# Hybrid attention layer on one core: one list of epilogue steps, two vector operations exchanged between engines, earlier weight requests

## The chip, the core and the metric

The kernel runs on one core of a Trainium2 chip. The metric is the device time of one execution in microseconds (us); lower is better. Five queues work side by side: TensorE (PE: matmuls and transposes), VectorE (DVE), ScalarE (ACT), GpSimd (POOL) and SyncE (SP), which here only requests DMA transfers. Each takes its instructions in a fixed order, and an instruction that waits holds up all that stand behind it in its queue.

## The reference, cut to what matters

```python
hdn = rmsnorm(x, norm_gain)                       # x: 2048 tokens x 1024
q_a, k_a, v_a, g_a, q_b, k_b, v_b, g_b = split(hdn @ w_in)
q, k = rope(rmsnorm(q, gain)), rope(rmsnorm(k, gain))      # both mixers, per head
o_a = banded_attention(q_a, k_a, v_a, 127, sinks) * silu(g_a)      # 8 heads, 2 kv heads
o_b = dilated_attention(q_b, k_b, v_b) * silu(g_b)  # 3 patterns, merged by their denominators
out = x + concat(o_a, o_b) @ w_out
```

## The kernel before, in words

The projections run in eight stages (`STAGES`): B0 to B3 (two heads of the dilated mixer each), A0 and A1 (four heads of the window mixer each), O0 and O1 (half the output columns each). A stage goes over the 2048 tokens in four blocks `sb`, a block in two halves of 256 tokens, a half in two tiles `tt` of 128. Every product is made of three matmuls, since weights and activations are split into a high and a low part. `proj` makes q, k and v of a tile in one PSUM tile `pj` (two buffers), then the gates of the half.

After each q/k/v tile, `norm_rope` squares and reduces on ACT and DVE (`un`, L413), multiplies by the cosine and sine tables on DVE out of PSUM (L420 and L422 for B, L427 and L429 for A), adds the two products on POOL (L431, the rotary sum) and, as the last reader of `pj`, writes the low part of V on DVE (L311). After both tiles of a half, `norm_factors` makes the norm factors `fac` on POOL (L437, L182). `norm_split` multiplies the rotated q and k by `fac` on DVE (L447), rounds them on ACT (L456, L457) and subtracts on POOL (L458, L459), which gives `hl`. The transposes of `hl` come in the next half.

The attention work is cut into units of three or four steps (`scores`, `transposes`, `pv`, `after`). `advance` calls the next step, and the loop at the end spreads these calls over the matmuls of the projections by the cost noted with each step. The softmax denominators go to DRAM (`rD`, `rA`) and come back broadcast over the partitions (`Rb`, one buffer); POOL multiplies the attention outputs `osum` with them: `final` for the window mixer (L686, L688), `first`, `second` and `third` for the dilated one (L899, L904, L905, L906). These late pieces stand in the list `late` with a count of `tick` calls, each entry counting by itself.

`w_tiles` loads a stage's weights through three staging buffers (`stg`): `main(c)` and `gate(c)` request a block (L118, L131) and split it on ACT and DVE (L101 and L102, L104 and L105). They are called from the matmul loops of the last half of the stage before.

The order of the program is not the order of the queues. The launch builds the program with

```python
with tile.TileContext(nc, schedule_with_timeline_sim=True) as tc:
```

so that, when it is built, the instructions of each queue are put in order along a simulated timeline; the place in the program then decides between instructions that could both go.

Of the kernel before, what the change touches and what calls it, by code (L numbers as in the profile page):

```python
# [9 lines left out]
F32 = mybir.dt.float32  # L10
# [8 lines left out]
KC = DM // 128  # L19
# [4 lines left out]
SB = 3  # L24
BIG = 1e30
STAGES = [("B", 0), ("B", 1), ("B", 2), ("B", 3), ("A", 0), ("A", 1), ("O", 0), ("O", 1)]

# [6 lines left out]
def hybrid_layer(ctx, tc, xT, xn, x, wB, wA, wO, ng, gains, sinks, rot, masks, ident, out):  # L34
# [72 lines left out]
    def w_tiles(si):  # L107
        kind, idx = STAGES[si]
        src = {"B": wB, "A": wA, "O": wO}[kind][idx]
        nm = 256 if kind == "O" else 384  # L110
        q, g = [], []

        def main(c, then=None):
            if si == 0:
                f = wk.tile([128, nm], F32, name=("cq", "ck", "cv")[c % 3])
            else:
                f = xp.tile([128, nm], F32, name="stg", bufs=SB)
            nc.sync.dma_start(f, src[:, c, :nm])  # L118
            h = wp.tile([128, nm], F32R, name="wh", bufs=WB)
            l = wp.tile([128, nm], F32R, name="wl", bufs=WB)  # L120
            if then:
                then()
            split_w(kind, c, f, h, l)
            q.append((h, l))

        def gate(c):
            k = 2 if kind == "B" else 1
            if c % k:
                return
            f = xp.tile([128, k, 256 // k], F32, name="stg", bufs=SB)  # L130
            nc.sync.dma_start(f, src[:, c:c + k, nm:])  # L131
# [5 lines left out]
        return q, g, main, gate  # L137


# [106 lines left out]
    def proj(si, sb):  # L246
# [22 lines left out]
        for half in range(2):  # L269
# [8 lines left out]
            for tt in range(2):  # L278
# [98 lines left out]
    deferred = []  # L377
    late = []

    tabs = {}  # L380
# [25 lines left out]
    def norm_rope(kind, nq, nk, T, tt, pj, TC, TS, u, vt):  # L406
# [16 lines left out]
        for qk, m in enumerate((nq, nk) if kind == "A" else ()):  # L423
# [17 lines left out]
    def norm_split(kind, nq, nk, t1s, fac):  # L441
# [74 lines left out]
    def proj_out(si, sb, wq, wg, last):  # L516
# [4 lines left out]
        for half in range(2):  # L521
# [6 lines left out]
            for tt in range(2):  # L528
# [6 lines left out]
                for n in range(2 * KC):  # L535
# [5 lines left out]
                    if o == 0:  # L541
                        continue
                    if last and half == 1 and tt == 1:
                        W[si + 1][2](c)
                        W[si + 1][3](c)
# [110 lines left out]
    def units_A(si, sb):  # L656
# [21 lines left out]
        def final(p):  # L678
            d = osum["d", p]
            rb = wk.tile([128, 512], F32, name="Rb", bufs=1)  # L680
            for a in range(2):
                nc.sync.dma_start(rb[64 * a:64 * a + 64, :],
                                  bass.AP(tensor=d.tensor, offset=d.offset + a * 512, ap=[[0, 64], [1, 512]]))
            t = osum[p]
            g = G[si, sb][p].rearrange("p r i u -> p (r i u)")
            nc.gpsimd.tensor_tensor(t, t, g, op=OP.mult)  # L686
            mix = wk.tile([128, 512], F32, name="o1c", bufs=1)
            nc.gpsimd.tensor_tensor(cm_view(mix), cm_view(t), to_cm(rb), op=OP.mult)  # L688
            for a in range(2):
                nc.sync.dma_start(mx[2 * sb + a][:, 2 * idx + p, :], mix[:, 256 * a:256 * a + 256])  # L690

# [7 lines left out]
    def pair_units(si, sb, p, sc, osum, rows, final):  # L699
# [7 lines left out]
        def scores(h):  # L707
            if h % 2 == 0:
                osum[p] = wk.tile([128, 512], F32, name="osum", bufs=3)
            s[h] = window_scores(si, sb, h, [sc[:, 0, h, i:i + 1] for i in range(4)], [sc[:, 1, h, i:i + 1] for i in range(4)])  # L710
# [31 lines left out]
        def after():  # L742
            rows(p)
            late.append([5, lambda: final(p)])

# [4 lines left out]
    def units_B(si, sb):  # L750
        sc = wk.tile([128, 4, 2, 2], F32, name="scB")
        osum = wk.tile([128, 512], F32, name="osum", bufs=3)
        d = spill_tiles(si)
        units = []
        for h in range(2):
            def after(h=h):
                if h == 1:
# [4 lines left out]
                    cs = slice(sb * 128, sb * 128 + 128)  # L762
                    nc.sync.dma_start(d["o"][:, :, cs].rearrange("r p c -> p r c"), osum.rearrange("p (r c) -> p r c", r=4))
            stats = ([sc[:, i, 0, h:h + 1] for i in range(4)], [sc[:, i, 1, h:h + 1] for i in range(4)])
            units.append(window_unit(si, sb, h, stats, cm_view(osum[64 * h:64 * h + 64, :]), after))
# [5 lines left out]
    def units_D(si, r):  # L771
# [4 lines left out]
        def dil(h):  # L776
# [61 lines left out]
            def pv():  # L838
# [11 lines left out]
                if h == 0:  # L850
                    c["o2"] = wk.tile([128, 512], F32, name="osum", bufs=3)
                evac_o(po, c["o2"][hp:hp + 64, :])

            def after():
# [26 lines left out]
                nc.sync.dma_start(dd, rr)  # L881
                o1 = wk.tile([128, 512], F32, name="o1c", bufs=1)
                nc.sync.dma_start(o1, d["o"][r])
                gc = wk.tile([128, 512], F32, name="gc", bufs=1)
                nc.sync.dma_start(gc, d["g"][r])
                o2 = c["o2"]
                def bcast(k):
# [4 lines left out]
                    return rb  # L892

                def first():
                    rb = bcast(0)
                    late.append([3, lambda: second(rb)])

                def second(rb):
                    nc.gpsimd.tensor_tensor(o1, o1, rb, op=OP.mult)  # L899
                    rb = bcast(1)  # L900
                    late.append([3, lambda: third(rb)])

                def third(rb):
                    nc.gpsimd.tensor_tensor(o2, o2, rb, op=OP.mult)  # L904
                    nc.gpsimd.tensor_tensor(o2, o2, o1, op=OP.add)  # L905
                    nc.gpsimd.tensor_tensor(o2, o2, gc, op=OP.mult)  # L906
# [133 lines left out]
```

## Time and profile before

| | |
|---|---|
| median of 3 runs | 1259.9 us (1255.32 to 1261.03) |
| the profiled execution: its time | 1261.51 us |
| the profiled execution: its span | 1259.4 us |
| mean granted clock of TensorE | 0.969 of full speed |
| TensorE busy | 1174.8 us, 8328 matmuls |
| VectorE, ScalarE, GpSimd busy | 850.7, 834.7, 680.4 us |

All durations below are from the profiled execution; the span is 2.1 us shorter than its time. Matmuls overlap, so a busy TensorE is not one at its peak: the count of matmuls in a stretch says more than the busy share. The clock is given as a share of the full 2.4 GHz; a mean between 0.5 and 1 over a stretch means that part of it was granted at 1.2 GHz.

### The profile page before, as it was taken

The page shows a single profiled execution, that of the slowest core. Times are in us where ns is not written, and L with a number is a line of the kernel's source. Part 1 is how long each engine was busy: PE and PEld are TensorE (multiplying, and loading weights), DVE is VectorE, ACT ScalarE, POOL GpSimd, SP SyncE. Part 2 cuts the span into 40 slices and gives each one's busy share as a digit, 9 for nine tenths or more (in the row PEclk, how much of TensorE's full clock was granted, in tenths as well). Part 3 has the DMA queues.
Part 4 walks back from the last instruction along what each step waited for, and adds up shares of the span by engine and source line. Part 5 has one row for each costly group of instructions (what it writes and reads, how often), then busy time and mean ns, then how long its engine had stood idle before and what let it go on. Part 6 is the DMA issues. An engine that isn't in the chain of part 4 may idle for free.

```text
span 1259.4 us, 25438 instructions
## 1 busy us (share of the span) xinstructions
PE 1174.8 (93%) x8328; PEld 1141.3 (91%) x8328; DVE 850.7 (68%) x2288; ACT 834.7 (66%) x2418; POOL 680.4 (54%) x788
## 2 busy tenths in 40 slices
PE   6898979899899798899998999999999999999899
PEld 5898979899799798888997999898899998999898
DVE  5676768678677678776777788789868877522221
ACT  6477868678677687676777677677776776522221
POOL 4886734566645574536576567565655554333122
PEclk9899989999899899899998999999999999999999
DMA  7454677877687667687775764545333225566561
GB/s 215 120 166 127 193 226 212 229 200 212 182 250 207 210 190 201 189 244 204 199 210 172 228 203 143 150 137 167 114 97 94 80 89 165 163 192 211 166 191 69
DMA packets 196883, 220.98 MB, mean 175 GB/s; under 512 B 34312, under 2 KB 143632, under 8 KB 196752
## 3 DMA queue, kind: packets, MB, share of 16 engines
q1 hardware_dynamic: 196752, 219.37, 59.3%
q8 instruction: 66, 1.08, 0.4%
q14 instruction: 65, 0.53, 0.1%
HBM read 164.44 MB, written 54.86 MB: 174 GB/s over the span
## 4 chain that ended last, share of the span: by engine, by line
PE 55%; DMA 16%; DVE 10%; ACT 8%; POOL 6%; issue 3%; SPq 2%; POOLq 0%; ACTq 0%; DVEq 0%
PE pj L244 39%; DMA xs<-in_xT 3%; DMA Rb<-rD 2%; DMA stg<-in_wB 2%; PE po L849 2%; DMA stg<-in_wO 2%; DMA stg<-in_wA 2%; PE sc L590 1%; PE sc L591 1%; PE po L645 1%; PE pt L828 1%; PE po L735 1%; PE pt L719 1%; ACT P L599 1%; DVE ptl L574 1%
## 5 line engine op out<-in xcount | busy, mean ns | idle before, releaser
L244 PE MATMUL pj<-wh,xh 128*128 128x384 f32 (+1 forms) x1008 | 332.8, 332 | 12.2 <-ACT wh L104 5.5
L244 PE MATMUL pj<-wl,xh 128*128 128x384 f32 (+1 forms) x1008 | 334.4, 332 | 0.8 <-DVE wl L102 0.7
L244 PE MATMUL pj<-wh,xl 128*128 128x384 f32 (+1 forms) x1008 | 333.4, 331 | 1.3 <-DVE xl L157 1.3
L157 POOL TENSOR_TENSOR xl<-xs,xh 128x512 fp32r<-128x512 f32 x158 | 210.3, 1341 | 146.3 <-ACT xh L155 136.6
L155 ACT ACTIVATE xh<-xs 128x512 fp32r<-128x512 f32 x252 | 154.5, 629 | 123.6 <-PE pj L244 100.6
L244 PEld LDWEIGHTS pj<-wh,xh 128*128 128x128 f32 x1008 | 194.0, 193 | 15.7 <-ACT wh L104 5.8
L244 PEld LDWEIGHTS pj<-wl,xh 128*128 128x128 f32 x1008 | 194.8, 193 | 3.2 <-DVE wl L102 1.1
L244 PEld LDWEIGHTS pj<-wh,xl 128*128 128x128 f32 x1008 | 194.4, 193 | 3.0 <-DVE xl L157 1.6
L574 DVE TENSOR_TENSOR ptl<-pt,pth 128x512 fp32r<-128x512 f32 (+3 forms) x232 | 142.0, 619 | 35.5 <-ACT pth L573 31.8
L244 PE MATMUL pj<-xh,wgh 128*128 128x256 f32 x496 | 147.7, 298 | 17.9 <-DVE V L311 12.0
L244 PE MATMUL pj<-xh,wgl 128*128 128x256 f32 x496 | 145.8, 294 | 0.0
L244 PE MATMUL pj<-xl,wgh 128*128 128x256 f32 x496 | 145.4, 293 | 0.0
L573 ACT ACTIVATE pth<-pt 128x512 fp32r<-128x512 f32 (+3 forms) x232 | 123.1, 543 | 23.1 <-PE pt L719 8.1
L431 POOL TENSOR_TENSOR t<-t,t 128x256 f32<-128x256 f32 (+1 forms) x96 | 78.1, 814 | 77.9 <-DVE t L422 57.2
L244 PEld LDWEIGHTS pj<-xh,wgh 128*128 128x128 f32 x496 | 97.8, 197 | 19.7 <-ACT klz L502 5.9
L244 PEld LDWEIGHTS pj<-xl,wgh 128*128 128x128 f32 x496 | 97.8, 197 | 0.6
L244 PEld LDWEIGHTS pj<-xh,wgl 128*128 128x128 f32 x496 | 97.4, 196 | 0.9 <-DVE wgl L105 0.2
L814 ACT ACTIVATE P<-P,scD 128x256 f32<-128x256 f32 (+3 forms) x128 | 71.6, 560 | 33.6 <-DVE scD L813 32.9
L157 DVE TENSOR_TENSOR xl<-xs,xh 128x512 fp32r<-128x512 f32 x94 | 76.9, 823 | 21.1 <-ACT xh L155 20.5
L447 DVE TENSOR_TENSOR t<-t,fac 128x256 f32<-128x256 f32 (+1 forms) x96 | 67.4, 710 | 30.8 <-POOL fac L182 23.7
L182 POOL TENSOR_TENSOR fac<-un,mhalf 128x8 f32<-128x8 f32 (+1 forms) x48 | 85.4, 1779 | 2.5
L813 DVE CUSTOM_DVE_ANT_0 P<-sc,mk 128x256 f32<-128x256 f32 (+3 forms) x128 | 61.1, 484 | 32.2 <-PE sc L809 31.5
(188 smaller groups left out, 3082.8 us busy)
## 6 DMA issues: line engine op xcount, KB each, us to landing
xs<-in_xT SPq DMA_DIRECT2D x94, 512.0 KB
xs<-mx SPq DMA_DIRECT2D x32, 512.0 KB
vd<-V SPq DMA_DIRECT2D x64, 128.0 KB
qd<-qc SPq DMA_DIRECT2D x32, 256.0 KB
TT<-tab SPq DMA_DIRECT2D x32, 256.0 KB
cv<-vd SPq DMA_DIRECT2D x32, 256.0 KB
cq<-qd SPq DMA_DIRECT2D x32, 256.0 KB
ck<-kd SPq DMA_DIRECT2D x64, 128.0 KB
```

The source lines that it names most:

```text
L155: nc.scalar.activation(h, f, AF.Copy)
L157: eng.tensor_tensor(l, f, f32(h), op=OP.subtract)
L182: nc.gpsimd.tensor_tensor(y, u, mhalf.to_broadcast([128, n]), op=OP.pow)
L244: nc.tensor.matmul(o, a, b, start=first and n == 0, stop=last and n == 2, skip_group_check=True)
L431: nc.gpsimd.tensor_tensor(t1[:, :n], t1[:, :n], t2[:, :n], op=OP.add)
L447: nc.vector.tensor_tensor(t1v, t1v, fac[:, tt, :, None].to_broadcast([128, nh, 64]), op=OP.mult)
L573: nc.scalar.activation(hi, pt, AF.Copy)
L574: nc.vector.tensor_tensor(lo, pt, f32(hi), op=OP.subtract)
L590: nc.tensor.matmul(sc[:, j, :], q[h // 2][:, h % 2, i, :], kw, start=True, stop=False)
L813: nc.vector.tensor_tensor_reduce(pd, o[:, :m], m2[:, 512 - m:], -0.125, BIG, OP.add, OP.min, nb)
L814: nc.scalar.activation(pd, pd, AF.Exp, bias=nb, scale=-1.0, accum_out=l)
L849: nc.tensor.matmul(po[:, o:o + w], a, b, start=n_ == 0, stop=n_ == len(seq) - 1, skip_group_check=True)
```

## The change

Three edits. (1) The rotary sum L431 goes from POOL to DVE, and the multiplication by `fac` L447 from DVE to POOL. (2) Every attention epilogue becomes an entry of short steps in one list; only the head of the list counts down, one step at a time; the loads of `o1` and `gc` move from `after` into the first step, the stores to `mx` into a last step of their own, two ticks after the last multiplication. `osum_tile` runs steps of the list at once when three `osum` tiles are in use. (3) The request of a weight block is taken out of `main` and `gate`: `prime` requests the first three blocks in the tile before, and each split is followed by the request of the block three further on; the order of the blocks and the three buffers stay.

```diff
+        def load(n):
+            if n >= len(order) or order[n] in staged:
+                return
+            part, c = order[n]
...
+                f = xp.tile(shape, F32, name="stg", bufs=SB)
+            nc.sync.dma_start(f, src[:, c, :nm] if part == "m" else src[:, c:c + k, nm:])
+            staged[order[n]] = f
+        def prime():
+            for n in range(SB):
+                load(n)
         def main(c, then=None):
-            nc.sync.dma_start(f, src[:, c, :nm])
+            f, n = take("m", c)
             h = wp.tile([128, nm], F32R, name="wh", bufs=WB)
...
             split_w(kind, c, f, h, l)
             q.append((h, l))
+            if si:
+                load(n + SB)
...
+                    if last and half == 1 and tt == 0 and c == 3:
+                        W[si + 1][4]()                     # prime
                     if last and half == 1 and tt == 1:
                         W[si + 1][2](c)                    # main
...
+    def step():
+        late[0].pop(0)[1]()
+        if not late[0]:
+            late.pop(0)
+    def osum_tile():
+        while live[0] >= OS and late:
+            step()
+        live[0] += 1
+        return wk.tile([128, 512], F32, name="osum", bufs=OS)
...
-        nc.gpsimd.tensor_tensor(t1[:, :n], t1[:, :n], t2[:, :n], op=OP.add)
+        nc.vector.tensor_tensor(t1[:, :n], t1[:, :n], t2[:, :n], op=OP.add)
...
-            nc.vector.tensor_tensor(t1v, t1v, fac[:, tt, :, None].to_broadcast([128, nh, 64]), op=OP.mult)
+            nc.gpsimd.tensor_tensor(t1v, t1v, fac[:, tt, :, None].to_broadcast([128, nh, 64]), op=OP.mult)
...
-            late.append([5, lambda: final(p)])             # window mixer
+            late.append([[1, load], [4, scale], [2, store]])
...
-                late.append([2, first])                    # dilated: then 3 to second, 3 to third
+                late.append([[1, first], [4, second], [4, third], [1, fourth], [2, store]])
...
     def tick():
-        for ent in late[:]:
-            ent[0] -= 1
-            if ent[0] <= 0:
-                late.remove(ent)
-                ent[1]()
+        if late:
+            late[0][0][0] -= 1
+            if late[0][0][0] <= 0:
+                step()
```

## Rows read from the trace of the kernel before

**Rows 1.** The page, part 1: busy us, share of the span, instructions.
```profile
PE 1174.8 (93%) x8328; PEld 1141.3 (91%) x8328; DVE 850.7 (68%) x2288; ACT 834.7 (66%) x2418; POOL 680.4 (54%) x788
```

**Rows 2.** Stretches of 20 us: busy (instructions) per engine, granted clock, DMA share, GB/s.
```profile
core 0: us, PE busy (x) PEld busy (x) DVE busy (x) ACT busy (x) POOL busy (x), PEclk, DMA share, GB/s
240.00:260.00 20.00, 16.77 (x107) 15.68 (x106) 12.40 (x30) 13.11 (x37) 16.34 (x20) 0.91 0.81 225
400.00:420.00 20.00, 17.34 (x110) 16.45 (x109) 13.19 (x31) 12.74 (x41) 12.73 (x14) 0.91 0.77 220
420.00:440.00 20.00, 14.98 (x95) 14.46 (x94) 11.35 (x31) 11.88 (x36) 14.77 (x20) 0.83 0.71 214
440.00:460.00 20.00, 20.00 (x144) 19.65 (x143) 15.15 (x41) 17.08 (x48) 12.55 (x15) 1.00 0.77 213
580.00:600.00 20.00, 17.35 (x112) 16.43 (x111) 14.72 (x33) 12.08 (x36) 12.48 (x14) 0.91 0.73 214
600.00:620.00 20.00, 18.24 (x115) 17.58 (x114) 14.40 (x45) 14.27 (x46) 10.22 (x14) 0.91 0.85 238
...
160.00:180.00 20.00, 13.55 (x92) 13.12 (x91) 14.02 (x43) 15.42 (x47) 8.38 (x11) 0.83 0.70 205
```

**Rows 3.** Timeline of POOL, 408 to 437 us: start, us, instruction [idle before <-releaser].
```profile
418.34 1.29 POOL L899 TENSOR_TENSOR o1c<-o1c,Rb 128x512 f32<-128x512 f32 x1 [7.27 <-DMA Rb<-rD]
...
424.69 1.29 POOL L904 TENSOR_TENSOR osum<-osum,Rb 128x512 f32<-128x512 f32 x1 [1.88 <-DMA Rb<-rD]
...
429.70 1.66 POOL L182 TENSOR_TENSOR fac<-un,mhalf 128x8 f32<-128x8 f32 x1
431.31 2.68 POOL L157 TENSOR_TENSOR xl<-xs,xh 128x512 fp32r<-128x512 f32 x2
```

**Rows 4.** Timeline of DVE, 428 to 436 us.
```profile
431.39 2.88 DVE L447 TENSOR_TENSOR t<-t,fac 128x256 f32<-128x256 f32 x2 [5.71 <-POOL fac L182]
```

**Rows 5.** Timeline of PE, 428 to 436 us.
```profile
434.79 1.11 PE L828 MATMUL pt<-idf,P 128*128 128x128 f32 x4 [5.02 <-DVE ptl L574]
```

**Rows 6.** Waits of the whole span: us in total, times, longest us.
```profile
DVE t L447 <- POOL fac L182: 23.7, 9, 5.7
...
PE pj L244 <- DVE V L311: 13.2, 7, 5.7
...
ACT hl L456 <- DVE t L447: 11.9, 10, 3.0
...
DVE t L447 <- POOL t L431: 6.8, 2, 6.6
```

**Rows 7.** Groups by line: count | busy us, mean ns of one | idle before.
```profile
L431 POOL TENSOR_TENSOR t<-t,t 128x256 f32<-128x256 f32 (+1 forms) x96 | 78.1, 814 | 77.9 <-DVE t L422 57.2
L447 DVE TENSOR_TENSOR t<-t,fac 128x256 f32<-128x256 f32 (+1 forms) x96 | 67.4, 710 | 30.8 <-POOL fac L182 23.7
```

**Rows 8.** Groups of POOL by line, the table products.
```profile
L396 POOL TENSOR_TENSOR TT<-TT,gt 128x128 f32<-128x128 f32 x64 | 34.1, 553 | 32.4 <-DMA TT<-in_rot 32.4
```

**Rows 9.** Line 447 alone: duration ns minimum/median/maximum, first and last start.
```profile
L447 DVE TENSOR_TENSOR t<-t,fac x96: 403/536/1510, 44.6 to 1045.2; 128x256 f32<-128x256 f32 x64, 128x320 f32<-128x320 f32 x32
```

**Rows 10.** Timeline of SP, 160 to 200 and 300 to 312 us: weight requests.
```profile
162.17 4.22 SPq L118 DMA_DIRECT2D stg<-in_wB  x3
189.76 0.43 SPq L118 DMA_DIRECT2D stg<-in_wB  x1
...
307.60 2.44 SPq L118 DMA_DIRECT2D stg<-in_wB  x3
```

**Rows 11.** Timeline of ACT, 303 to 312 us: the splits of B2's weights.
```profile
305.04 1.12 ACT L104 ACTIVATE wh<-stg,ngt 128x384 fp32r<-128x384 f32 x2
...
310.94 1.12 ACT L104 ACTIVATE wh<-stg,ngt 128x384 fp32r<-128x384 f32 x2 [2.19 <-DMA stg<-in_wB]
```

**Rows 12.** Waits of SP over the span.
```profile
SPq L118 <- DVE wl L105: 9.1, 12, 2.2
```

**Rows 13.** Timeline, 923 to 935 us: an epilogue of the window mixer.
```profile
926.58 0.28 SPq L675 DMA_DIRECT2D rA<-rr  x1
927.80 1.09 SPq L682 DMA_DIRECT2D Rb<-rA  x2
```

More of the change, by code (lines that the diff above doesn't have):

```diff
@@ L25 @@
 BIG = 1e30
+OS = 3
 STAGES = [("B", 0), ("B", 1), ("B", 2), ("B", 3), ("A", 0), ("A", 1), ("O", 0), ("O", 1)]
@@ L110, in w_tiles, with take @@
         nm = 256 if kind == "O" else 384
-        q, g = [], []
-        def main(c, then=None):
[L114 to L117, printed above, removed]
-            nc.sync.dma_start(f, src[:, c, :nm])
+        k = 2 if kind == "B" else 1
+        q, g, staged = [], [], {}
+        mains, gates = [("m", c) for c in range(KC)], [("g", c) for c in range(0, KC, k)]
+        order = mains + gates
+        if si and STAGES[si - 1][0] == "O":
+            order = [w for pair in zip(mains, gates) for w in pair]
+        def load(n):
+            if n >= len(order) or order[n] in staged:
+                return
+            part, c = order[n]
+            shape = [128, nm] if part == "m" else [128, k, 256 // k]
+            if si == 0 and part == "m":
+                f = wk.tile(shape, F32, name=("cq", "ck", "cv")[c % 3])
+            else:
+                f = xp.tile(shape, F32, name="stg", bufs=SB)
[4 more added lines that the diff above has]
+                load(n)
+        def take(part, c):
+            n = order.index((part, c))
+            load(n)
+            return staged[part, c], n
+        def main(c, then=None):
+            f, n = take("m", c)
             h = wp.tile([128, nm], F32R, name="wh", bufs=WB)
@@ L124, in main @@
             q.append((h, l))
+            if si:
+                load(n + SB)
         def gate(c):
-            k = 2 if kind == "B" else 1
             if c % k:
                 return
-            f = xp.tile([128, k, 256 // k], F32, name="stg", bufs=SB)
-            nc.sync.dma_start(f, src[:, c:c + k, nm:])
+            f, n = take("g", c)
             h = wp.tile([128, k, 256 // k], F32R, name="wgh", bufs=8)
@@ L136, in gate @@
                 g.append((h[:, j], l[:, j]))
-        return q, g, main, gate
+            if si:
+                load(n + SB)
+        return q, g, main, gate, prime
     XG = {}
@@ L378, in hybrid_layer, with osum_free @@
     late = []
+    live = [0]
+    def step():
[7 more added lines that the diff above has]
+        return wk.tile([128, 512], F32, name="osum", bufs=OS)
+    def osum_free():
+        live[0] -= 1
     tabs = {}
@@ L542, in proj_out @@
                         continue
+                    if last and half == 1 and tt == 0 and c == 3:
+                        W[si + 1][4]()
                     if last and half == 1 and tt == 1:
@@ L678, in final, with load, scale, store @@
         def final(p):
[L679 to L683, printed above, removed]
-            t = osum[p]
[L685 to L690, printed above, removed]
+            t = osum[p]
+            def load():
+                d = osum["d", p]
+                rb = osum["r", p] = wk.tile([128, 512], F32, name="Rb", bufs=1)
+                for a in range(2):
+                    nc.sync.dma_start(rb[64 * a:64 * a + 64, :],
+                                      bass.AP(tensor=d.tensor, offset=d.offset + a * 512, ap=[[0, 64], [1, 512]]))
+                nc.gpsimd.tensor_tensor(t, t, G[si, sb][p].rearrange("p r i u -> p (r i u)"), op=OP.mult)
+            def scale():
+                mix = osum["m", p] = wk.tile([128, 512], F32, name="o1c", bufs=1)
+                nc.gpsimd.tensor_tensor(cm_view(mix), cm_view(t), to_cm(osum["r", p]), op=OP.mult)
+            def store():
+                for a in range(2):
+                    nc.sync.dma_start(mx[2 * sb + a][:, 2 * idx + p, :], osum["m", p][:, 256 * a:256 * a + 256])
+                osum_free()
+            late.append([[1, load], [4, scale], [2, store]])
         for p in range(2):
@@ L708, in scores @@
             if h % 2 == 0:
-                osum[p] = wk.tile([128, 512], F32, name="osum", bufs=3)
+                osum[p] = osum_tile()
             s[h] = window_scores(si, sb, h, [sc[:, 0, h, i:i + 1] for i in range(4)], [sc[:, 1, h, i:i + 1] for i in range(4)])
@@ L751, in units_B @@
         sc = wk.tile([128, 4, 2, 2], F32, name="scB")
-        osum = wk.tile([128, 512], F32, name="osum", bufs=3)
+        osum = osum_tile()
         d = spill_tiles(si)
@@ L850, in pv @@
                 if h == 0:
-                    c["o2"] = wk.tile([128, 512], F32, name="osum", bufs=3)
+                    c["o2"] = osum_tile()
                 evac_o(po, c["o2"][hp:hp + 64, :])
@@ L892, in bcast, with second, third, fourth @@
                     return rb
+                rbs = []
                 def first():
[L895 to L906, printed above, removed]
+                    o1 = wk.tile([128, 512], F32, name="o1c", bufs=1)
+                    nc.sync.dma_start(o1, d["o"][r])
+                    gc = wk.tile([128, 512], F32, name="gc", bufs=1)
+                    nc.sync.dma_start(gc, d["g"][r])
+                    rbs.extend([o1, gc, bcast(0)])
+                def second():
+                    nc.gpsimd.tensor_tensor(rbs[0], rbs[0], rbs[2], op=OP.mult)
+                    rbs.append(bcast(1))
+                def third():
+                    nc.gpsimd.tensor_tensor(o2, o2, rbs[3], op=OP.mult)
+                    nc.gpsimd.tensor_tensor(o2, o2, rbs[0], op=OP.add)
+                def fourth():
+                    nc.gpsimd.tensor_tensor(o2, o2, rbs[1], op=OP.mult)
+                def store():
                     ch = 4 + STAGES[si][1]
```

7 lines of the change are left out of this document (3 added, 4 removed).

## The prediction

> **What bounds the kernel now.** Read the busy shares first: TensorE is busy 93% of the span, no other engine reaches 70% [rows 1]. That looks bound by TensorE, but busy matmuls overlap, so read next the stretches of 20 us and count matmuls. Where nothing disturbs a B stage, 144 of them start in 20 us, 0.139 us each, at the full granted clock; in the disturbed stretches only 92 to 115 start and the mean clock falls to 0.91 or 0.83 [rows 2], that is, part of the stretch ran at 1.2 GHz after TensorE had stood still. So (144 minus the count) times 0.139 us is what a disturbance costs, clock included: 4.7 and 6.8 us for the two stretches from 400 to 440, 4.4 and 4.0 for 580 to 620, together 20.0; 5.1 for 240 to 260; 7.2 for 160 to 180, which is a change of stage [rows 2]. The mix of matmuls differs a little from stretch to stretch, so each is good to perhaps half a microsecond.
>
> What makes such a hole is seen in the timelines around 430 us. POOL stands 7.27 us and then 1.88 us before two epilogue products, because the broadcast denominators have not landed; the norm factors stand behind them and come out at 431.36 [rows 3]. DVE has its multiplication by those factors at the head of its queue, waits 5.71 us for them, and then needs 2.88 us for the pair, while POOL runs its own two-input subtractions from 431.31 on [rows 3, 4]. A split of transposed scores stands behind that pair on DVE, and TensorE waits 5.02 us for it [rows 5]. Over the span DVE waits 23.7 us for the factors and 6.8 us for the rotary sum [rows 6], 30.5 in all. The reader is to see one pattern: a late DMA holds POOL, POOL holds DVE, DVE holds TensorE. If the four stretches of 400 to 440 and 580 to 620 are all put down to it, which I choose to do, a microsecond of DVE's wait costs 20.0 / 30.5 = 0.66 us of time.
>
> **The change, part by part.** (a) The exchange takes the multiplication by the factors off DVE. Nothing on DVE then waits for `fac` or for the rotary sum, which follows its own two products on DVE. The whole 20.0 us hang on this wait. But ScalarE's rounding, which waited 11.9 us for the multiplication on DVE [rows 6], will now wait for it on POOL, behind the same late products, and ScalarE too holds work for TensorE. Ends: nothing gained (ScalarE takes DVE's place) and 20.0. I take two thirds, 13.3 us, because ScalarE's rounding has the transposes of the next half as its only use, whereas the pair on DVE stood right before work that TensorE asked for [rows 4, 5].
>
> (b) The rotary sum, now on DVE, stands between the table products and V's low part, which is the last reader of the PSUM tile. TensorE waits for that release 7 times, 13.2 us [rows 6]; there every nanosecond counts, elsewhere the second PSUM buffer hides it. The trace has no such sum on DVE; the nearest row is the removed multiplication, the same shapes with two SBUF inputs, 403 ns at least, 536 median, 1510 at most [rows 9]. 7 times 0.54 is 3.8 us lost; ends 0 and 10.6. On busy time it is a fair exchange for DVE, which gives up 67.4 us [rows 7] for 96 times 0.54, 51 us; DVE is not the bound.
>
> (c) On POOL 96 sums of 814 ns, 78.1 us [rows 7], go, and 96 products with a broadcast factor come. The plain sum has the same shapes, hence 814 ns and no difference; the other end is the table product with a broadcast operand, 553 ns for 128 elements [rows 8], which for the mean of 277 elements makes 1.20 us and 37 us more in all. POOL stands idle for 579 us of the span [rows 1], so neither end sets the time by itself. What hides the later `hl` is the time until the next half's transposes; without that cover it is the slower rival below. A rule speaks against this edit: the Trainium skill, GPSIMD Engine Reference, section Engine selection, sends elementwise work with two inputs to VectorE, as about twice as slow on GpSimd. The rows show 814 against 710 ns as means, since DVE's own is stretched [rows 7], and nearly a factor of two only against DVE's shortest, 403 ns [rows 9]. By the rule on the mean the products would take 1.42 us, 58 us more on POOL than now, still inside its idle time, and the sum would not move; it makes the slower rival dearer.
>
> (d) The weight requests. The program asks for a block where it is split, but the queue does not: a request for B2's weights goes out at 189.76 us, the next ones only at 307.60, after the first splits of that stage at 305.04 [rows 10, 11]. So the first three blocks are in the buffers 115 us ahead already, and `prime` can give nothing. The later requests stand at the head of SP's queue until a staging buffer is given back, 12 times for a main block of the B and A stages, 9.1 us [rows 12]: they cannot go out earlier without a fourth buffer, and the change keeps three. I take 0. Ends: 2 us lost, one wait of 2.2 [rows 12] of SP before a transfer that is needed, and 11 gained, a quarter of the 7.2 us at each of six later changes of stage, if ScalarE's splits find their blocks sooner.
>
> (e) The list. The counts of ticks are places in the program, and the queues don't keep to them either: the window mixer's broadcast is to come five ticks after its row is stored, some 4.3 us of attention steps by the program's own costs of 853 to 870 ns; it goes out 1.2 us after the store was requested, as soon as that can have landed [rows 13]. One, four or five ticks more or less then decide only between instructions that are ready together. I take 0; ends 5.1 gained (the stretch from 240, where the same products are late [rows 2]) and 4.8 lost: an epilogue that has to go through 12 ticks in place of 8 holds the one behind it, and one more wait of 7.27 us [rows 3] is passed on at 0.66.
>
> Sum against the profiled execution: 1261.5 - 13.3 + 3.8 = 1252.0 us. The median of the runs shown is 1.6 us below that execution, so I predict 1250 us, 0.8% faster.
>
> **The rivals.** *Larger gain.* The exchange gives all 20.0 us, the later stores and multiplications also clear the stretch from 240 (5.1), and the splits find their weights (11): 36.1 less, nothing lost on V: 1224 us. For it: the three holes have one pattern, and SP is blocked by stores that wait for POOL in the old form. Against: (d) and (e) say that the places in the program bind little.
>
> *The change does nothing to the path.* ScalarE waits where DVE waited, V's delay and small gains cancel: 1260 us. For it: the cause, the late broadcast, is not touched; Rb keeps one buffer and the two round trips to DRAM follow each other as before.
>
> *Slower.* Place: POOL's queue between the factors and `hl`. Today only the subtractions stand there after ScalarE's rounding; now two products of 0.81 us stand in front, 1.6 us a half, and POOL, which serves ScalarE and waits for it in turn, is late with the activations' low parts as well. ScalarE inherits DVE's wait, so the 20.0 us stay; if a quarter of the 48 halves pass the 1.6 us on to TensorE, 19.5 come on top, and V's 3.8: 1261.5 + 23.3 - 1.6 = 1283 us. It decides the sign from 8 halves on, whose 13 us eat the gain of (a). For it: four stretches already show POOL as the late engine. Against: POOL is busy 54% only [rows 1].
>
> **How the numbers follow.** A difference under 0.5%, 6.3 us, is about what a measurement of this kernel can tell from no change. Forecast (1236 to 1256) 0.41; larger gain (below 1236) 0.16; nothing (1256 to 1266) 0.22; slower (above 1266) 0.21. A tenth of the forecast's weight lies above 1253.6. Faster 0.53, same 0.26, slower 0.21. For 8 in 10 the range goes to the larger gain's 1224 and half-way from no change to the slower rival, 1272; some 0.06 lies below and 0.14 above. Cases of both signs hold most of the chance, so the likeliest one's own range, 1236 to 1256, stands beside it. All queues are put in order anew when the program is built, and that alone can move single holes of 4 to 7 us; it is why no case is given more.
>
> **What would show it.** Right: no wait of DVE for `fac`; the stretches with products by Rb hold 130 matmuls or more in 20 us; L447 on POOL at 0.75 to 0.9 us; the first three weight blocks of a stage landing long before their splits, as now; TensorE's waits for V longer by 3 to 4 us. Wrong: ScalarE waiting 30 us or more for L447 and TensorE for ScalarE behind it (slower, or nothing); TensorE waiting for `hl`; or holes at the changes of stage gone, which would mean that the requests did matter and (d) is mis-sized.

## The result, and the profile after

| | before | after |
|---|---|---|
| median (13 runs each) | 1259.03 us | 1266.77 us |
| lowest to highest | 1252.07 to 1266.68 us | 1258.0 to 1269.7 us |
| ratio after to before, 95% interval | | 1.0049 [1.0025, 1.0073] |
| the profiled execution: time, span | 1261.51, 1259.4 us | 1258.13, 1256.4 us |

The changed kernel is 0.5% slower, where 0.8% faster was forecast (the ratio is not the quotient of the two medians). The times after fall in two groups, six from 1258.0 to 1261.9 us and seven from 1266.8 to 1269.7, and the profile is of the first group: it tells where the waits are, but not what the 0.5% is. The lines of the program have moved: L431 is now L473, L447 is L489, L458 is L500, L456 is L498, L475 is L517, L899 and L904 are L953 and L957, L688 is L735, L311 is L338, L244 is L269.

The busy shares, the page's part 1 of after (columns as in [rows 1]):

```profile
PE 1168.8 (93%) x8328; PEld 1135.5 (90%) x8328; DVE 845.4 (67%) x2288; ACT 836.5 (67%) x2418; POOL 670.9 (53%) x788
```

Nothing here tells the two kernels apart: the work has only changed places. The stretches of 20 us do (columns as in [rows 2]):

```profile
240.00:260.00 20.00, 16.16 (x104) 15.24 (x103) 10.87 (x32) 11.62 (x33) 14.33 (x18) 0.91 0.72 210
400.00:420.00 20.00, 19.88 (x145) 19.37 (x144) 13.59 (x34) 14.70 (x43) 13.61 (x16) 1.00 0.75 211
420.00:440.00 20.00, 16.76 (x102) 15.98 (x101) 14.59 (x41) 13.09 (x42) 13.49 (x17) 0.91 0.74 198
440.00:460.00 20.00, 18.31 (x131) 17.85 (x130) 13.43 (x35) 15.31 (x43) 8.94 (x10) 1.00 0.72 193
460.00:480.00 20.00, 17.41 (x106) 17.07 (x107) 10.97 (x36) 14.49 (x44) 15.97 (x21) 0.83 0.64 178
580.00:600.00 20.00, 19.43 (x134) 18.81 (x133) 14.96 (x38) 13.40 (x39) 14.69 (x18) 1.00 0.77 228
600.00:620.00 20.00, 18.95 (x133) 17.60 (x131) 12.15 (x39) 15.13 (x46) 11.65 (x16) 1.00 0.85 227
620.00:640.00 20.00, 16.90 (x124) 16.47 (x124) 13.57 (x35) 15.31 (x43) 12.85 (x16) 1.00 0.53 154
640.00:660.00 20.00, 17.91 (x122) 17.01 (x121) 16.76 (x45) 14.17 (x43) 12.41 (x18) 1.00 0.71 217
...
160.00:180.00 20.00, 15.40 (x101) 15.34 (x102) 13.70 (x43) 15.80 (x47) 7.94 (x11) 0.83 0.70 201
```

By the prediction's own count (144 less the matmuls, times 0.139 us), 400 to 440 lost 11.5 us before and loses 5.7 now; but 440 to 480, which lost nothing in its first half before [rows 2], now loses 1.8 and 5.3. The stretch from 240 loses 5.6 where it lost 5.1. So from 400 on the holes have moved by some 40 us and are no smaller, 12.8 us for 11.5. From 580 to 620 the count gives 2.9 us lost, where it was 8.4, but the next 40 us, beyond the stretches that the prediction priced, lose 5.8. What ends them is told by the waits of the whole span (us in total, times, longest us), to be read against [rows 6]:

```profile
POOL o1c L735 <- DMA Rb<-rA: 49.6, 13, 6.8
POOL o1c L953 <- DMA Rb<-rD: 43.4, 13, 7.3
POOL osum L957 <- DMA Rb<-rD: 36.9, 9, 10.5
...
ACT hl L498 <- POOL t L489: 24.7, 10, 5.2
...
PE pj L269 <- DVE V L338: 13.9, 7, 5.6
PE po L517 <- POOL hl L500: 13.7, 9, 4.3
```

No wait of VectorE for `fac` is left, of 23.7 us. In its place ScalarE's rounding waits 24.7 us, for the product that is now on GpSimd (before, 11.9 us, for the product on VectorE), and the transposes of `hl` on TensorE wait 13.7 us for the subtraction on GpSimd. In the kernel before that last wait was a single one; this line of its waits, and those of GpSimd for the denominators, did not stand ahead:

```profile
POOL o1c L899 <- DMA Rb<-rD: 58.3, 15, 8.2
POOL o1c L688 <- DMA Rb<-rA: 26.7, 10, 5.7
...
POOL osum L904 <- DMA Rb<-rD: 16.8, 7, 4.9
...
PE po L475 <- POOL hl L458: 2.6, 1, 2.6
```

So GpSimd's waits for the broadcasts have not become shorter either: 101.8 us before, 129.9 after, three lines each.

One hole shows the mechanism. First the last of the half's four roundings, which are the subtraction's input, in ScalarE's timeline of after, then GpSimd's own timeline (start, us, instruction, [idle before <-releaser]):

```profile
453.16 0.40 ACT L499 ACTIVATE hl<-t 128x256 fp32r<-128x256 f32 x1
```

```profile
453.68 1.30 POOL L953 TENSOR_TENSOR o1c<-o1c,Rb 128x512 f32<-128x512 f32 x1 [6.99 <-DMA Rb<-rD]
...
456.18 0.73 POOL L521 CAST qc<-Q 128x256 fp32r<-128x256 f32 x2
460.87 1.26 POOL L957 TENSOR_TENSOR osum<-osum,Rb 128x512 f32<-128x512 f32 x1 [3.96 <-DMA Rb<-rD]
462.09 0.45 POOL L500 TENSOR_TENSOR hl<-t,hl 128x128 fp32r<-128x128 f32 x1
```

The rounding of both tiles is done at 453.56. The subtractions need nothing more, and the first starts at 462.09, 8.5 us later: GpSimd works for some 3.4 us of these and then stands 3.96 us, because L957 is ahead of the subtraction in its queue and waits for a transfer. TensorE's timeline of after shows who pays, and SyncE's when the two broadcasts were requested:

```profile
462.59 0.75 PE L517 MATMUL po<-idr,hl 128*128 128x128 f32 x4 [4.29 <-POOL hl L500]
```

```profile
450.06 1.14 SPq L939 DMA_DIRECT2D Rb<-rD  x2
...
455.73 1.10 SPq L939 DMA_DIRECT2D Rb<-rD  x2
```

There is one `Rb` buffer, so the second broadcast goes out only when the first product, which ends at 454.98, has read the first one; it is in use 5.1 us after its request. The wait of 6.99 us before the first product is not one for the buffer: there SyncE itself waits 3.8 us, until the denominators have landed in DRAM, before it requests them back. TensorE stands 4.29 us, and in the stretch from 460 the mean granted clock is 0.83, so part of that stretch ran at 1.2 GHz.

### The profile page after: what moved, and what is told of

The parts are those of the page before. It is cut to its first block, busy times and chain, and to the rows that moved or that the text cites. A ratio compares the mean times of both kernels' runs of the same rounds, so it can differ in the third digit from the quotient of the medians.

```text
span 1256.4 us, 25495 instructions
## 1 busy us (share of the span) xinstructions
PE 1168.8 (93%) x8328; PEld 1135.5 (90%) x8328; DVE 845.4 (67%) x2288; ACT 836.5 (67%) x2418; POOL 670.9 (53%) x788
## 4 chain that ended last, share of the span: by engine, by line
PE 61%; DMA 15%; POOL 7%; ACT 7%; DVE 6%; issue 3%; SPq 1%; POOLq 0%; DVEq 0%; ACTq 0%
PE pj L269 42%; DMA stg<-in_wB 3%; DMA stg<-in_wA 2%; PE po L902 2%; DMA xs<-in_xT 2%; DMA Rb<-rD 2%; PE pt L771 2%; PE po L689 2%; PE sc L634 2%; PE po L787 2%; PE sc L635 1%; POOL xl L182 1%; PE sc L861 1%; PE pt L881 1%; PE sc L862 1%
## 5 line engine op out<-in xcount | busy, mean ns | idle before, releaser
L269 PE MATMUL pj<-wh,xh 128*128 128x384 f32 (+1 forms) x1008 | 333.5, 333 | 11.7 <-ACT wh L105 5.7
L269 PE MATMUL pj<-wh,xl 128*128 128x384 f32 (+1 forms) x1008 | 331.8, 330 | 0.6 <-DVE xl L182 0.6
L269 PE MATMUL pj<-wl,xh 128*128 128x384 f32 (+1 forms) x1008 | 331.5, 329 | 0.7 <-DVE wl L103 0.7
L269 PEld LDWEIGHTS pj<-wh,xh 128*128 128x128 f32 x1008 | 193.0, 192 | 15.4 <-ACT wh L105 5.7
L269 PEld LDWEIGHTS pj<-wl,xh 128*128 128x128 f32 x1008 | 193.3, 192 | 3.0 <-DVE wl L103 1.1
L269 PEld LDWEIGHTS pj<-wh,xl 128*128 128x128 f32 x1008 | 193.2, 192 | 2.3 <-DVE xl L182 0.8
L269 PE MATMUL pj<-xh,wgh 128*128 128x256 f32 x496 | 146.9, 296 | 11.8 <-DVE V L338 11.8
L269 PE MATMUL pj<-xl,wgh 128*128 128x256 f32 x496 | 146.2, 295 | 0.0
L269 PE MATMUL pj<-xh,wgl 128*128 128x256 f32 x496 | 146.1, 295 | 0.0
L269 PEld LDWEIGHTS pj<-xh,wgh 128*128 128x128 f32 x496 | 97.7, 197 | 13.4 <-issue 5.8
L269 PEld LDWEIGHTS pj<-xl,wgh 128*128 128x128 f32 x496 | 97.7, 197 | 0.6
L269 PEld LDWEIGHTS pj<-xh,wgl 128*128 128x128 f32 x496 | 97.8, 197 | 0.4
L182 DVE TENSOR_TENSOR xl<-xs,xh 128x512 fp32r<-128x512 f32 x94 | 81.4, 872 | 19.8 <-ACT xh L180 19.2
L867 ACT ACTIVATE P<-P,scD 128x128 f32<-128x128 f32 (+3 forms) x128 | 71.6, 560 | 22.1 <-DVE scD L866 21.6
L479 POOL TENSOR_TENSOR un<-un,eps 128x8 f32<-128x8 f32 (+1 forms) x48 | 10.6, 221 | 130.3 <-DVE un L455 127.7
L489 POOL TENSOR_TENSOR t<-t,fac 128x256 f32<-128x256 f32 (+1 forms) x96 | 68.9, 730 | 19.7 <-DVE t L473 15.3
L455 DVE TENSOR_REDUCE un<-sq 128x4 f32<-128x256 f32 (+1 forms) x96 | 42.0, 437 | 50.6 <-ACT sq L452 49.4
```

What stands on the lines that cost most here:

```text
L182: eng.tensor_tensor(l, f, f32(h), op=OP.subtract)
L269: nc.tensor.matmul(o, a, b, start=first and n == 0, stop=last and n == 2, skip_group_check=True)
L455: nc.vector.tensor_reduce(uv, sq[:, :n].rearrange("p (h d) -> p h d", d=64), axis=AX.X, op=OP.add)
L489: nc.gpsimd.tensor_tensor(t1v, t1v, fac[:, tt, :, None].to_broadcast([128, nh, 64]), op=OP.mult)
L867: nc.scalar.activation(pd, pd, AF.Exp, bias=nb, scale=-1.0, accum_out=l)
```

## The experiments

All ran in five rounds beside the kernel before. Ratios are to the kernel before on the same chip, with the 95% interval; "swap" is edit (1) alone.

| run | what it is | median us (before) | ratio |
|---|---|---|---|
| e1_exchange | before + swap | 1258.48 (1256.48) | 1.0015 [0.9995, 1.0035] |
| e2_list | before + edit (2) | 1258.95 (1256.48) | 1.0004 [0.9982, 1.0026] |
| e3_loads | before + edit (3) | 1257.18 (1256.48) | 1.0002 [0.9981, 1.0022] |
| e4_sum_only | before + sum on VectorE | 1275.96 (1256.48) | 1.0139 [1.0109, 1.0169] |
| e5_mult_only | before + product on GpSimd | 1263.40 (1258.08) | 1.0056 [1.0024, 1.0087] |
| e6_replan | before, one planner cost changed | 1257.45 (1258.08) | 1.0003 [0.9980, 1.0026] |
| e7_before_norb | before, `Rb` not read | 1271.57 (1258.08) | 1.0116 [1.0084, 1.0147] |
| e8_exchange_norb | swap, `Rb` not read | 1246.66 (1258.08) | 0.9926 [0.9898, 0.9955] |
| e9_before_nodma | before, products read no transfer | 1243.65 (1256.74) | 0.9898 [0.9867, 0.9929] |
| e10_exchange_nodma | swap, products read no transfer | 1239.96 (1256.74) | 0.9848 [0.9813, 0.9883] |
| e11_exchange_rb2 | swap, two `Rb` | 1232.64 (1256.74) | 0.9805 [0.9775, 0.9835] |
| e12_exchange_behind | swap, late products behind `hl` | 1246.74 (1256.74) | 0.9914 [0.9882, 0.9946] |
| e13_before_rb2 | before, two `Rb` | 1238.03 (1259.58) | 0.9827 [0.9797, 0.9858] |
| e14_after_rb2 | after, two `Rb` | 1239.07 (1259.58) | 0.9832 [0.9797, 0.9867] |
| e15_exchange_t2one | swap, one `t2` (control) | 1254.59 (1259.58) | 0.9964 [0.9938, 0.9989] |
| e16_rb2_behind | swap, two `Rb`, behind `hl` | 1229.28 (1259.58) | 0.9759 [0.9728, 0.9791] |
| e17_before_t2one | before, one `t2` (control) | 1261.62 (1255.95) | 1.0046 [1.0022, 1.0069] |
| e18_before_rb2_behind | before, two `Rb`, behind `hl` | 1230.56 (1255.95) | 0.9800 [0.9772, 0.9828] |

### Each edit alone, and the order of the queues alone

```diff
e1: -        nc.gpsimd.tensor_tensor(t1[:, :n], t1[:, :n], t2[:, :n], op=OP.add)
    +        nc.vector.tensor_tensor(t1[:, :n], t1[:, :n], t2[:, :n], op=OP.add)
    -            nc.vector.tensor_tensor(t1v, t1v, fac[:, tt, :, None].to_broadcast([128, nh, 64]), op=OP.mult)
    +            nc.gpsimd.tensor_tensor(t1v, t1v, fac[:, tt, :, None].to_broadcast([128, nh, 64]), op=OP.mult)
e2: -            late.append([5, lambda: final(p)])
    +            late.append([[1, load], [4, scale], [2, store]])
...
e3: +                    if last and half == 1 and tt == 0 and c == 3:
    +                        W[si + 1][4]()
...
e6: -                    yield 490
    +                    yield 480
```

> The kernel before with the exchange alone (rotary sum on DVE, multiplication by fac on POOL). Theory A (the exchange gives and takes: DVE no longer waits for fac, TensorE waits for hl instead): within 5 us of the kernel before, no wait of DVE for fac, TensorE's waits for hl 8 us or more where they were 2.6. Theory B (the exchange gains, the list or the requests eat it): 8 to 15 us faster than before, TensorE's waits for hl below 6 us.

> The kernel before with the list of epilogue steps alone. Theory A: within 4 us of the kernel before; POOL's waits for Rb about the 102 us of before, DVE's waits for fac 15 to 35 us. Theory B (the list costs, because one entry holds the next): 8 to 15 us slower, POOL's waits for Rb 120 us or more.

> The kernel before with the earlier weight requests alone. Theory A (the queue had them early already): within 4 us of the kernel before; first three blocks of a stage requested over 100 us ahead of their splits in both, ScalarE's waits for weight blocks within 10 us of before's 48. Theory B (the order of the requests matters): 5 us or more away, to either side, and the waits for weight blocks move with it.

> The kernel before with the same instructions, laid out by another plan: a projection step counts 480 in place of 490 when attention steps are spread. A control: if laying the queues out anew moves the time by itself, it differs by 4 us or more; if not, it is within 3 us.

None of the three edits moves the time by itself beyond its interval, nor does the one other plan of the queues that was tried (e6). So (d) and (e) at nothing are borne out, each by its own run with an interval of about 0.2% to either side. The swap removes VectorE's wait for `fac`, as in the whole change, and gains nothing that shows. The waits of e1 over the span show why:

```profile
POOL o1c L688 <- DMA Rb<-rA: 46.8, 12, 8.7
POOL o1c L899 <- DMA Rb<-rD: 34.8, 13, 5.8
...
POOL osum L904 <- DMA Rb<-rD: 19.0, 8, 4.9
...
PE po L475 <- POOL hl L458: 14.8, 6, 5.0
PE pj L244 <- DVE V L311: 6.7, 6, 3.4
```

The wait of TensorE for `hl` is there with the swap alone, 14.8 us, so it comes with edit (1), not with the list. The releases of V are less late than before (6.7 for 13.2 us).

### The two halves of the swap

e4 takes the first pair of lines of e1's diff, e5 the second.

> The kernel before with only the rotary sum moved to DVE; the multiplication stays on DVE. Theory A (POOL's lateness is what counts, and POOL has 78 us less to do): 3 to 10 us faster; DVE still waits for fac, but less than 23.7 us; TensorE's waits for hl stay below 5 us. Rival (the sum delays V, and DVE is the fuller engine): 3 to 8 us slower, TensorE's waits for V above 17 us.

> The kernel before with only the multiplication by fac moved to POOL; the rotary sum stays on POOL, so POOL has some 70 us more to do. If the halves of the exchange simply add (sum on DVE was measured 18 us slower, both together 2 us): 12 to 18 us faster than before. If POOL's lateness is what counts: 3 to 15 us slower, TensorE's waits for hl above the 14.8 us of the exchange.

Both are slower alone, by 1.4% and 0.6%, and together they are not: the halves don't add up. Neither case put on record for e4 came: it is 19 us slower, where 3 to 10 faster or 3 to 8 slower was expected. With the sum alone on VectorE the old chain grows (waits of e4):

```profile
DVE t L447 <- POOL fac L182: 37.7, 14, 5.9
```

It was 23.7 us; the trace does not tell how much of this is VectorE's larger load and how much another order of the queues. With the product alone on GpSimd the new chain is there (waits of e5):

```profile
ACT hl L456 <- POOL t L447: 17.6, 8, 5.6
...
PE po L475 <- POOL hl L458: 12.0, 6, 3.3
```

So the wait for `hl` belongs to the product's move to GpSimd. e5's time, 5 us slower, fits its second case, but the wait for `hl` is 12.0 us, not above e1's 14.8 as was expected with it.

### Taking the late broadcast away

```diff
e7, e8:  -    nc.gpsimd.tensor_tensor(o1, o1, rb, op=OP.mult)
         +    nc.gpsimd.tensor_tensor(o1, o1, gc, op=OP.mult)
...
e9, e10: -    nc.gpsimd.tensor_tensor(o1, o1, rb, op=OP.mult)
         +    nc.gpsimd.tensor_tensor(o2, o2, gt.rearrange("p a b c d -> p (a b c d)"), op=OP.mult)
...
```

> The kernel before, but the epilogue products read the gate tile in place of the broadcast denominators, so POOL never waits for Rb (the denominators are still sent and fetched; the output lacks the normalization). Theory A (the late Rb is the root of the holes): 12 to 25 us faster, DVE's waits for fac below 8 us. Rival (POOL is late anyway): within 5 us, DVE's waits for fac above 15 us.

> The exchange alone with the same products by the gate tile. Theory A (the late Rb reaches TensorE through hl in place of DVE): 8 to 20 us faster than before, TensorE's waits for hl below 5 us. Rival (hl is late because two products stand before it on POOL, whatever Rb does): within 5 us of the exchange's time, hl waits above 10 us.

> The kernel before, its epilogue products on POOL reading a constant tile in place of the broadcast denominators, the stored first output and the gates, so that none of them waits for a transfer (all transfers are still made; the output lacks normalization, merge and gates of the dilated mixer). Theory A (late transfers at the head of POOL's queue make the holes): 10 to 25 us faster than before, DVE's waits for fac below 10 us. Rival (POOL would be late anyway): within 5 us, DVE's waits for fac above 15 us.

> The exchange alone with the same constant operands. Theory A (in the exchange the late transfers reach TensorE through hl): 10 to 25 us faster than before, TensorE's waits for hl below 5 us, and about as fast as the kernel before with constant operands, since then nothing is left for the exchange to decouple. Rival: 5 us or more faster than that one, because DVE is freed in any case.

e7 did not take the wait away but made another one, since the gate's tile comes by a transfer too (waits of e7):

```profile
POOL o1c L899 <- DMA gc<-gd: 57.4, 9, 11.3
```

As a test of the broadcast it is void. It tells something else: with this wait on GpSimd in both, the kernel with the swap is 25 us faster than the one without (1246.66 to 1271.57), and VectorE has no wait for `fac` in e8, since the product is on GpSimd there. So the swap can pay where GpSimd is held in this way; it did not with the broadcast as it was. e9 and e10, whose products read a constant tile, are the better test: 13 us faster than before without the swap, 17 with it. VectorE's wait for `fac` falls to 5.7 us in e9, and no matmul of TensorE waits for `hl` in e10, so both outlets close when GpSimd waits for no transfer. The intervals of the two ratios overlap, but both ran on one chip, and there all six times of e10 (1231.69 to 1241.97) lie under all six of e9 (1242.84 to 1251.31); the medians are 3.7 us apart, the means 6.4. So without transfers in GpSimd's way the swap does gain, some 4 to 6 us. That is about the border of the two cases put on record for e10, as fast as e9 or 5 us and more faster.

### Two Rb buffers

```diff
-    rb = wk.tile([128, 512], F32, name="Rb", bufs=1)
+    rb = wk.tile([128, 512], F32, name="Rb", bufs=2)
-    t2 = wk.tile([128, 320], F32, name="t2", bufs=2)
+    t2 = wk.tile([128, 320], F32, name="t2", bufs=1)
```

The second `Rb` needs SBUF space, which one `t2` buffer gives up; e15 and e17 have the `t2` line alone.

> The exchange with two buffers for the broadcast denominators (and one for t2, which DVE now both makes and reads), so the second broadcast need not wait for the first product. If the second wait for Rb is what makes hl late (three of the four largest holes stand behind L904): 4 to 10 us faster than before, POOL's waits of L904 for Rb below 8 us, TensorE's waits for hl below 8 us. If not: within 3 us of the exchange.

> The kernel before with two buffers for Rb and one for t2, no exchange. If the second buffer alone gives the gain: 18 to 26 us faster than before. If exchange and buffer need each other (DVE stays bound to POOL, and with one t2 DVE also waits for POOL's sum): between 8 us faster and 8 us slower, DVE's waits for fac and for the sum together 20 us or more.

> The whole change with two buffers for Rb and one for t2. If the list and the requests bind nothing: within 4 us of the exchange with two Rb buffers, 1233 us, so 20 to 28 us faster than before. If they cost the 4 to 8 us that lie between the exchange alone and the whole change: 13 to 19 us faster than before.

> The exchange with one buffer for t2 and still one for Rb. A control: within 4 us of the exchange alone, so about the time of the kernel before; TensorE's waits for hl 8 us or more. If the gain came from t2: 15 us or more faster.

> Control: the kernel before with one t2 buffer in place of two, one Rb buffer. If the 22 us that two Rb buffers gave on the kernel before belong to the buffer, this runs within 0.5% of before (1253 to 1266 us) or slower, since t2's second product then waits for the rotary sum on GpSimd. If it was t2 that gained, by another order of the queues, it runs at 1245 us or less.

With the second buffer the ratio falls from 1 to 0.9827 on the kernel before, from 1.0015 to 0.9805 with the swap, and from 1.0049 to 0.9832 on the whole change. For e11, 24 us faster, only 4 to 10 was expected. The controls show that `t2` is not the cause: alone it costs 0.5% without the swap and gives 0.4% with it. These two controls part by 0.8%, and their intervals do not touch: with one `t2` the swap gains. The two requests now follow each other before either product has run, in SyncE's timeline of e11 and then GpSimd's:

```profile
397.75 1.16 SPq L890 DMA_DIRECT2D Rb<-rD  x2
399.59 1.15 SPq L890 DMA_DIRECT2D Rb<-rD  x2
```

```profile
401.99 1.29 POOL L899 TENSOR_TENSOR o1c<-o1c,Rb 128x512 f32<-128x512 f32 x1 [6.62 <-DMA Rb<-rD]
...
404.89 1.29 POOL L904 TENSOR_TENSOR osum<-osum,Rb 128x512 f32<-128x512 f32 x1 [1.26 <-DMA Rb<-rD]
```

The two requests are 1.84 us apart where after had 5.67 (450.06 to 455.73), the products 2.9 us apart where after had 7.2. In the kernel before with two buffers, VectorE's wait falls from 23.7 to 8.7 us without any swap (waits of e13):

```profile
POOL o1c L899 <- DMA Rb<-rD: 57.0, 13, 7.0
POOL o1c L688 <- DMA Rb<-rA: 34.0, 12, 5.1
...
DVE t L447 <- POOL fac L182: 8.7, 8, 2.2
...
POOL osum L904 <- DMA Rb<-rD: 3.9, 3, 2.2
```

What GpSimd waits for the broadcasts in all has hardly changed, 94.9 us where it was 101.8; what goes is the wait of the second product, L904, 3.9 us where it was 16.8. SyncE, too, stood in the kernel before at the requests for the one `Rb`, with its later requests behind it (its waits, before):

```profile
SPq L890 <- DMA Rb<-rD: 9.1, 8, 3.0
...
SPq L890 <- POOL o1c L899: 7.2, 6, 1.4
```

In e13 neither line is left. No run tells how much of the 1.7% came through GpSimd's queue and how much through SyncE's.

### Late products behind the subtraction

```diff
+    def behind():
+        return tc.issue_after(SPLIT[0])
...
-                    nc.gpsimd.tensor_tensor(o2, o2, rb, op=OP.mult)
+                    with behind():
+                        nc.gpsimd.tensor_tensor(o2, o2, rb, op=OP.mult)
...
```

`SPLIT[0]` is the last subtraction of `hl` given out so far, and what stands under `behind()` is queued after it. The same stands around the other epilogue products of GpSimd.

> The exchange with every epilogue product queued on POOL behind the last subtraction for hl that stands before it in the program, so that the place in the program binds. If the order on POOL makes hl late: 4 to 12 us faster than before, TensorE's waits for hl below 5 us, POOL's waits for Rb fewer than the 101 us of before. If the products only come later and hold something else: within 3 us or slower.

> The exchange with two Rb buffers, and the epilogue products queued behind the subtractions for hl. If both edits remove one and the same wait: within 4 us of the exchange with two Rb buffers. If they add: 1220 to 1228 us. If the later products hold the osum tiles: slower than 1240.

> Two Rb buffers, one t2 buffer and the epilogue products queued behind the last subtraction of hl, without the exchange. Theory that the exchange has no part in the gain: as fast as the same kernel with the exchange, 1225 to 1234 us. Rival, that moving the multiplication by fac off VectorE pays once the products are out of the way: 1236 us or more here, no faster than with two buffers alone (1238).

With the swap and one buffer, the order alone takes the ratio from 1.0015 to 0.9914, 1.0% or 12.7 us. All that is left of TensorE's waits for the subtractions (L462 and L463 in e12) is one line:

```profile
PE po L489 <- POOL hl L463: 0.4, 1, 0.4
```

That is the direct test of the cause: GpSimd still waits for its broadcasts, 97.5 us in three lines (42.1, 42.0 and 13.4) where e1 has 100.6, but `hl` no longer stands behind them. With two buffers, e16 is the best version, 2.4% under before, between the two cases put on record for it. The stretches from 240 and 400 hold their matmuls now, but holes are left, as from 320:

```profile
240.00:260.00 20.00, 20.00 (x145) 19.59 (x144) 14.79 (x47) 16.27 (x51) 9.61 (x14) 1.00 0.85 242
320.00:340.00 20.00, 17.19 (x103) 16.67 (x102) 13.74 (x41) 15.45 (x46) 12.28 (x15) 0.85 0.70 193
400.00:420.00 20.00, 20.00 (x143) 19.66 (x142) 14.78 (x47) 16.21 (x49) 12.75 (x15) 1.00 0.93 248
```

e18, the same without the swap, comes out at 0.9800 against 0.9759, with intervals that overlap. So where the products are out of the way five rounds show no gain of the swap, though one of some 0.5% is not excluded. The expectation's rival, 1236 us or more without the swap, is not borne out.

## Why the prediction was wrong, by its steps

The measured 1266.8 us lies inside the range given for 8 in 10, 1224 to 1272, but only because this range spans both signs; the likeliest case, 1236 to 1256, did not come, and nor did its mechanism.

**What bounds the kernel.** The pattern was read rightly: a late DMA holds GpSimd, and GpSimd holds an engine that TensorE waits for. But it was priced at the wrong link. 0.66 us for each microsecond of VectorE's wait took this wait as the cause; it was one of two outlets of a cause further back, the broadcasts that reach GpSimd late, the second of each pair because of the single `Rb`.

**(a), the step that failed.** -13.3 us were taken "because ScalarE's rounding has the transposes of the next half as its only use". e1 removed the wait for `fac` and came out at +0.15%, 1.9 us, where (a) and (b) made -9.5. The use was named rightly; whether `hl` would still come in time for it was not looked up. With VectorE no longer waiting, GpSimd reaches the same late products, and what stands behind them now is `hl`: TensorE's wait for it went from 2.6 us to 14.8 (e1) and 13.7 (after). Its cover, "the time until the next half's transposes", was used up in the hole above: 8.5 us from rounding to subtraction, 4.29 of them felt by TensorE. The cause of the late products was left as it was, and 12.7 us came back when they were put behind `hl`: e12 stands 10.0 us under before, close to the -9.5. That VectorE is better off without the product was not wrong in itself, as e9 and e10 show; the step that failed is that ScalarE and `hl` would pass on only a third of the 20.0 us.

**(b).** +3.8 us were to be seen in TensorE's waits for V. They were 13.2 us before, 13.9 after, 6.7 in e1, but 16.6 in e4, the sum alone: a cost of this size shows only there. The sum's price was right: 0.54 us were taken for it, and after's rows have a median of 472 ns (L473 below).

**(c).** The product on GpSimd is cheaper than assumed, not dearer: 814 ns were taken, 730 measured, and GpSimd's busy time fell from 680.4 to 670.9 us. So the price was no problem; the place in the queue was. The groups by line of after (count | busy us, mean ns | idle before):

```profile
L489 POOL TENSOR_TENSOR t<-t,fac 128x256 f32<-128x256 f32 (+1 forms) x96 | 68.9, 730 | 19.7 <-DVE t L473 15.3 <-PE sc L862 2.6
L473 DVE TENSOR_TENSOR t<-t,t 128x256 f32<-128x256 f32 (+1 forms) x96 | 56.6, 590 | 0.3
```

The rule of the Trainium skill that the prediction weighed (GPSIMD Engine Reference, section Engine selection: about twice as slow for two inputs) does not show as a factor of two here: in the mean the same product took 710 ns on VectorE before [rows 7] and 730 on GpSimd now, the same sum 814 on GpSimd before and 590 on VectorE now. At the shortest the product took 403 ns on VectorE [rows 9] and 603 on GpSimd (last section). By its price the product would have stayed inside GpSimd's idle time too; the harm came from the order in the queue.

**(d)** is right. Nothing came of the earlier requests (e3: 1.0002), and the first blocks lie in their buffers about as long as before: in SyncE's timeline of after the last of B2's first blocks is requested at 185.87 and the next ones at 305.61, after ScalarE's first splits of that stage:

```profile
185.87 0.35 SPq L128 DMA_DIRECT2D stg<-in_wB  x1
...
305.61 2.44 SPq L128 DMA_DIRECT2D stg<-in_wB  x3
```

```profile
303.48 1.11 ACT L105 ACTIVATE wh<-stg,ngt 128x384 fp32r<-128x384 f32 x2
```

The change of stage from 160 to 180 holds 101 matmuls, 92 before, a difference of 1.3 us; e1, without edit (3), holds 104 there, so it is not the requests' doing.

**(e)** is right for the list alone (e2: 1.0004). With the swap it may not be quite nothing: GpSimd's waits for `Rb` are 100.6 us in e1 and 129.9 in the whole change, the longest 10.5 in place of 8.7.

**The rivals.** "The change does nothing to the path" came nearest: it said that Rb keeps one buffer and that ScalarE takes VectorE's place, and it gave 1260 us. "Slower" named the right queue, GpSimd between the factors and `hl`, but the wrong thing in it: not the two products of 0.81 us, which cost less than that, but the epilogue products, which wait for transfers. The sign that would show it, "TensorE waiting for `hl`", is there, 9 times over 48 halves.

**What stays open.** What the swap is worth depends on what else is late: nothing that shows in e1, 0.8% with one `t2` (e15 to e17), 4 to 6 us without transfers (e9, e10), no gain shown with two `Rb`. Why one `t2` makes this difference no run tells; TensorE's waits for `hl` are there in e15 too, 11.9 us. The whole change is at 1.0049, the swap alone at 1.0015, with intervals that overlap; no run ties the difference to one wait. With two `Rb` the two are again not told apart (e14 0.9832, e11 0.9805). That e13 (0.9827) is faster than e9, whose products wait for no transfer (0.9898), was not expected. In e9 the broadcasts into the single `Rb` are still made, and SyncE still stands for them, before it can request anything else (its waits in e9):

```profile
SPq L890 <- DMA Rb<-rD: 24.7, 16, 3.2
```

That this makes the difference is argued, not shown. The order behind `hl` with one `Rb` and without the swap was not tried.

## What to carry to other kernels

Before a wait is moved off one engine, follow its chain back to what is late, and then list what else stands behind that late item in the same queue: here the product left VectorE, and `hl` took its place behind the same transfer. Where two transfers through one buffer are each followed by a product in a busy queue, a second buffer (here 1.7%, 22 us, for 2 KB a partition) is tried before any work is moved between engines. An instruction whose inputs are ready is better put ahead of one that waits for a transfer, and such an order can be written down (here 12.7 us, with the swap).

## What was not expected of the hardware

The product with a broadcast factor on GpSimd is no slower than the plain sum of the same shape was: 730 ns against 814 [rows 7]. And the shorter operation on VectorE varies much more. The durations of both in after (ns, minimum/median/maximum):

```profile
L473 DVE TENSOR_TENSOR t<-t,t x96: 404/472/1571, 35.1 to 1041.5; 128x256 f32<-128x256 f32 x64, 128x320 f32<-128x320 f32 x32
L489 POOL TENSOR_TENSOR t<-t,fac x96: 603/672/1253, 43.3 to 1043.4; 128x256 f32<-128x256 f32 x64, 128x320 f32<-128x320 f32 x32
```

VectorE's sum stretches to 3.9 times its shortest, GpSimd's product to 2.1 times; the forms are 256 and 320 elements, which accounts for a factor of 1.25 at most.
